# The 16 by 16 corners of the attention probabilities: turned on VectorE in 32 by 32 blocks instead of on TensorE, with GpSimd's low parts of weights in 128-column pieces

## The chip, the cores and the metric

One core of a Trainium2 chip runs the whole program. The metric is the device time of one execution in microseconds. Before the change it is 1282.98 us, the median of three runs (1282.68 to 1283.24).

## What is computed

Two layers of a decoder over 528 positions: 16 learned meta tokens and then 512 real ones, of width 1024. Each layer projects the normed input once and gives its columns to eight heads of forgetting attention (64 wide) and four heads of retention (128 wide); their outputs are joined, projected and added to h; a gated feed-forward of width 2816 follows. The part that matters here is the attention:

```python
def attend(q_blk, c_q, q_pos, k_, v_, c_k, k_pos):
    s = jnp.einsum('bhqd,bhkd->bhqk', q_blk, k_).astype(jnp.float32) * scale
    s = s + c_q[..., :, None] - c_k[..., None, :]
    s = jnp.where(k_pos[None, :] <= q_pos[:, None], s, -jnp.inf)
    p = jax.nn.softmax(s, axis=-1)
    return jnp.einsum('bhqk,bhkd->bhqd', p.astype(v_.dtype), v_)

meta_out = attend(...)      # the 16 meta queries, a block of their own
# the 512 real queries, in 4 blocks of 128
h = h + jnp.einsum('blc,cd->bld', mix, w_out)
```

A query sees the keys up to its own position. A block of 128 real queries begins at position 16 + 128 b, and key tiles of 128 begin at 0, 128, 256, 384 and 512. So query block b needs the key tiles 0 to b, and of key tile b + 1 only its first 16 keys, and those only for the last 16 queries of the block: a 16 by 16 corner, whose upper triangle is masked.

## The kernel before, in words

Activations lie with features on the 128 partitions and the 528 positions along the free axis. Every product is computed in three parts from operands that are split into a high part (rounded to a matmul format) and a low part (the rest): high x high, high x low, low x high. So weights and activations are split all the time, the high part by a copy on ScalarE and the low part by a subtraction on VectorE (`split`, L126 to L128).

**Weights.** `dense_steps` gives a projection of 128 output columns as eight steps, one for each slice of 128 inputs; a step is six matmuls of 264 columns (or three of 512). Weights come by DMA into `raw`, and `convert` (L150) splits them in halves of four slices, 128x512 elements each: ScalarE writes `whi` (L176), and GpSimd (in the jobs marked `pool`) or VectorE writes `wlo` (L177). It is called one job ahead, at steps 1 and 4 of the job before.

**Attention.** Heads go in four pairs g (s = 0, 1). `scores(s, b)` computes the scores of one query block into PSUM, adds the mask to the diagonal piece on VectorE (L496), subtracts the cumulated gates and takes the row minimum (L497, into the tile `pd` of this block; L502 joins two minima for block 3), and ScalarE takes the exponential in place (L510). The meta block, b = -1, exists in layer 0 alone and has its own tiles `pm`; `normalise` (L520) divides it by its sums.

`turn(s, b)` (L526) brings the probabilities into the form that the second product needs, keys on the partitions: TensorE transposes the 128-column tiles of the block against the identity into PSUM, up to four to a bank (L401 in `transpose_into`), and `split` writes `pth` on ScalarE (L127) and `ptl` on VectorE (L128), which are [key in tile, key tile, query]. Block b is turned in b + 2 tiles, the last of which holds only the corner; the columns behind it are zeros, written once per layer. So block 3 takes five transposes and two splits. The meta block takes one transpose of a whole 128x128 tile.

`product(s)` (L536) multiplies with the values (L544 for the meta queries, L552 for the real ones); key tile j is used for the queries from 128 j on.

**Order.** TensorE's order is written by hand: `merge` places the steps of attention and retention among the projections' steps, and `turn` stands three blocks behind `scores`. The other engines' instructions are put in order by a scheduler, except those that are pinned; each engine then runs its own list in order. Work on SBUF by GpSimd and VectorE goes on while TensorE multiplies.

Of the kernel before, what the change touches and what calls it, by code (L numbers as in the profile page):

```python
# [10 lines left out]
F32 = mybir.dt.float32  # L11
# [7 lines left out]
META = 16  # L19
T = SEQ + META  # L20
# [12 lines left out]
GAMMA = tuple(1.0 - 2.0 ** (-5 - h) for h in range(RH))  # L33
NEG = -1.0e30
HALF = T // 2


@with_exitstack
def hybrid_kernel(ctx, tc, x_t, w_in, w_fl, w_out, w_gate, w_up, w_down, vecs, b_fg, rope, decay, mask, ident, out_t):
    nc = tc.nc  # L40
# [22 lines left out]
    onec = const.tile([128, 1], F32, name="onec")  # L63
    nc.vector.memset(onec, 1.0)

    p_tiles, pm_tiles, v_tiles, end_tiles, low_keys = [], [], [], [], []
    rot = {"pm": 0}


# [10 lines left out]
    def enter_att(l):  # L80
        enter("att")
        low_keys[:] = [phase["att"].tile([128, T], F32R, name=f"kl{s}") for s in range(2)]
        for s, t in enumerate(low_keys):
            (nc.gpsimd if l else nc.vector).memset(t[64 * (1 - s):64 * (2 - s)].bitcast(F32), 0.0)

        for lst, n, cols, z0 in ((p_tiles, NBLK, None, None), (v_tiles, 2, TP, T)):
            lst[:] = [phase["att"].tile([128, cols or 128 * (i + 2)], F32, name=f"pd{z0}_{i}") for i in range(n)]
            for i, t in enumerate(lst):
                z = META + 128 * (i + 1) if z0 is None else z0
                zero(l, t[:, z:z + 128 - META])  # L90
        pm_tiles[:] = [phase["att"].tile([128, 128], F32, name=f"pm{i}") for i in range(2)] if l == 0 else []
        for t in pm_tiles:
            zero(l, t)
        end_tiles[:] = [[phase["att"].tile([128, META], F32R, name=f"rs{i}{k}") for k in range(2)] for i in range(2)]
        for t in end_tiles[0] + end_tiles[1]:
            zero(l, t.bitcast(F32))

    def zero(l, t):
        (nc.gpsimd if l else nc.vector).memset(t, 0.0)
# [50 lines left out]
    def convert(j, upto=NK, pinned=False):  # L150
# [18 lines left out]
        while job["split"] < min(n, upto):  # L169
            c0 = job["split"]  # L170
            c1 = min(n, c0 + (2 if j < 2 and c0 < 4 else 4))
            size, hi, lo = job["w"][c0 // job["w"][0][0]]
            o = c0 % size
            hi, lo = hi[:, o:o + c1 - c0], lo[:, o:o + c1 - c0]
            with tc.high_priority() if j == 5 else ExitStack():
                pin(nc.scalar.copy(hi, job["raw"][:, c0:c1]), pinned)  # L176
            pin(sub(lo, job["raw"][:, c0:c1], hi.bitcast(F32)), pinned)  # L177
# [112 lines left out]
    def pin(f, pinned=True):  # L290
        if pinned:
            tc.keep_in_program_order(f)
# [160 lines left out]
    def fox_steps(g, st, ly, real):  # L453
# [21 lines left out]
        def scores(s, b):  # L475
# [33 lines left out]
            pr = pt[0:nq, 0:nk]  # L509
            nc.scalar.activation(pr, pr, AF.Exp, bias=nmax[0:nq], scale=-1.0, accum_out=rsum)  # L510
# [69 lines left out]
        steps.append(lambda: product(1))  # L580
        cut = len(steps) - lag - 1
        return steps[:cut], steps[cut:]

    KOFF = (0, 128, 256, 384, SEQ)
    KLEN = (128, 128, 128, 128, META)
# [798 lines left out]
```

## Time and profile before

| | before |
|---|---|
| median of the runs | 1282.98 us |
| the profiled execution, first to last instruction (span) | 1282.4 us |
| TensorE busy | 1265.5 us, 9335 matmuls |
| VectorE busy | 1013.6 us, 1828 instructions |
| ScalarE busy | 691.4 us, 1246 instructions |
| GpSimd busy | 177.3 us, 145 instructions |

The profile is of one execution; no time of its own is given for it beside its span, which is 0.6 us below the median of the runs. PE is TensorE's matmul (a transpose is one too), PEld its weight load, DVE VectorE, ACT ScalarE, POOL GpSimd. Matmuls overlap, so the distance between the starts of two tells more than how long one lasts. A bracket behind a row of the timeline names how long the engine was idle before it, and what ended that.

### The profile page before, as it was taken

Reading aid. Unit: us, or ns where it says so; the run is one execution under the profiler, and the core shown is the slowest. Engines: PE = TensorE matmul, PEld = TensorE weight load, DVE = VectorE, ACT = ScalarE, POOL = GpSimd, SP = SyncE. Lnnn points to the kernel's source line nnn. Section 1 sums busy time; section 2 is a strip of 40 time slices with the busy share of each in tenths; the row PEclk is TensorE's granted clock in tenths of the full one; section 3 lists DMA queues with packets and bytes.
Section 4 is the critical chain, followed back from the end, with each engine's and each line's share of the span. In section 5 each row is a group of like instructions: output and inputs, shape, how many; then the busy total and the mean of one; then the engine's idle time right before and its main releaser. Section 6 shows DMA issues by size and latency. Waiting matters only on the chain.

```text
span 1282.4 us, 23297 instructions
## 1 busy us (share of the span) xinstructions
PE 1265.5 (99%) x9335; PEld 1205.4 (94%) x9335; DVE 1013.6 (79%) x1828; ACT 691.4 (54%) x1246; POOL 177.3 (14%) x145
## 2 busy tenths in 40 slices
PE   9999999999999999999999999999999999999997
PEld 8899999999999999999999989999789999999996
DVE  7877856879988887887686878568899878888866
ACT  6666655676444444444455665457765444444444
POOL 1233333210000000000014334333000000000000
PEclk9999999999999999999999999999999999999998
DMA  6222222123333333332323122222223322332321
GB/s 231 76 67 84 75 84 84 60 68 121 109 98 99 99 99 99 100 99 83 99 76 117 59 99 84 75 92 67 99 78 129 106 99 99 99 100 99 105 77 66
DMA packets 45676, 120.54 MB, mean 94 GB/s; under 512 B 5360, under 2 KB 12272, under 8 KB 45568
## 3 DMA queue, kind: packets, MB, share of 16 engines
q1 hardware_dynamic: 45136, 118.77, 28.2%
q8 instruction: 73, 1.20, 0.4%
q14 instruction: 35, 0.29, 0.1%
q10 hardware_dynamic: 432, 0.29, 0.1%
HBM read 116.91 MB, written 2.13 MB: 93 GB/s over the span
## 4 chain that ended last, share of the span: by engine, by line
PE 88%; DVE 7%; ACT 3%; DMA 1%; issue 1%; DVEq 0%; ACTq 0%
PE psd L200 27%; PE psa L860 18%; PE psd L995 14%; PE psd L860 13%; PE psa L995 4%; PE psa L200 4%; PE psa L401 2%; PE psa L490 2%; PE psa L552 1%; PE psa L709 1%; PE psa L679 1%; DMA bc<-cdr 1%; ACT whi L176 0%; DVE qs L421 0%; DVE kl L435 0%
## 5 line engine op out<-in xcount | busy, mean ns | idle before, releaser
L177 POOL TENSOR_TENSOR wlo<-raw,whi 128x512 fp32r<-128x512 f32 x126 | 171.8, 1377 | 386.0 <-ACT whi L176 384.8
L200 PE MATMUL psd<-xh,whi 128*128 128x264 f32 (+1 forms) x792 | 196.6, 316 | 0.8 <-ACT whi L176 0.8
L200 PE MATMUL psd<-xh,wlo 128*128 128x264 f32 (+1 forms) x792 | 187.2, 304 | 0.0
L200 PE MATMUL psd<-xl,whi 128*128 128x264 f32 (+1 forms) x792 | 186.5, 303 | 0.4 <-DVE xl L303 0.4
L200 PEld LDWEIGHTS psd<-xh,whi 128*128 128x128 f32 x792 | 128.9, 190 | 5.6 <-ACT whi L176 1.5
L200 PEld LDWEIGHTS psd<-xh,wlo 128*128 128x128 f32 x792 | 127.5, 189 | 6.4 <-DVE wlo L177 0.4
L200 PEld LDWEIGHTS psd<-xl,whi 128*128 128x128 f32 x792 | 128.2, 190 | 4.7 <-DVE xl L303 0.8
L176 ACT CAST whi<-raw 128x512 fp32r<-128x512 f32 (+1 forms) x168 | 98.2, 614 | 38.2 <-PE psd L200 18.0
L848 ACT CAST whi<-raw 128x1024 fp32r<-128x1024 f32 (+2 forms) x62 | 54.9, 885 | 51.3 <-PE psd L860 40.0
L848 ACT CAST fwhi<-raw 128x1024 fp32r<-128x1024 f32 (+2 forms) x62 | 55.6, 897 | 47.5 <-PE psd L860 40.0
L849 DVE TENSOR_TENSOR wlo<-raw,whi 128x1024 fp32r<-128x1024 f32 (+2 forms) x62 | 62.9, 1014 | 11.3 <-ACT whi L848 10.9
L849 DVE TENSOR_TENSOR fwlo<-raw,fwhi 128x1024 fp32r<-128x1024 f32 (+2 forms) x62 | 64.0, 1032 | 9.0 <-ACT fwhi L848 8.7
L860 PE MATMUL psa<-th,whi 128*128 128x264 f32 (+1 forms) x232 | 65.5, 282 | 0.0
L860 PE MATMUL psa<-th,wlo 128*128 128x264 f32 (+1 forms) x232 | 65.4, 282 | 0.0
L860 PE MATMUL psa<-tl,whi 128*128 128x264 f32 (+1 forms) x232 | 65.3, 282 | 0.0
L510 ACT ACTIVATE pdNone<-pdNone,nmax 128x144 f32<-128x144 f32 (+1 forms) x64 | 36.9, 576 | 50.4 <-DVE nmax L497 33.6
L860 PE MATMUL psa<-th,fwhi 128*128 128x264 f32 (+1 forms) x224 | 63.4, 283 | 0.0
L860 PE MATMUL psa<-tl,fwhi 128*128 128x264 f32 (+1 forms) x224 | 63.3, 283 | 0.0
L860 PE MATMUL psa<-th,fwlo 128*128 128x264 f32 (+1 forms) x224 | 63.3, 282 | 0.0
L128 DVE TENSOR_TENSOR ptl<-psa,pth 128x512 fp32r<-128x512 f32 (+4 forms) x88 | 41.9, 490 | 26.9 <-ACT pth L127 26.9
L926 ACT COPY e<-psa 128x264 f32<-128x264 f32 (+1 forms) x114 | 42.8, 375 | 28.4 <-PE psa L860 24.1
L848 ACT CAST fwhi<-S 128x1024 fp32r<-128x1024 f32 x20 | 21.0, 1049 | 68.6 <-PE psa L860 66.5
(339 smaller groups left out, 4031.7 us busy)
## 6 DMA issues: line engine op xcount, KB each, us to landing
raw<-w_in SPq DMA_DIRECT2D x54, 512.0 KB, 3.5
raw<-w_gate SPq DMA_DIRECT2D x44, 512.0 KB, 3.9
fraw<-w_up SPq DMA_DIRECT2D x38, 512.0 KB, 3.5
raw<-w_down SPq DMA_DIRECT2D x64, 256.0 KB, 2.7
raw<-w_out SPq DMA_DIRECT2D x16, 512.0 KB, 3.5
raw<-w_down SPq DMA_DIRECT2D x32, 192.0 KB, 2.4
bc<-cdr SPq DMA_DIRECT2D x16, 264.0 KB, 3.2
raw<-w_up SPq DMA_DIRECT2D x6, 512.0 KB, 3.4
```

What stands on the lines that cost most here:

```text
L128: pin(nc.vector.tensor_sub(lo, src, hi.bitcast(F32)), pinned)
L176: pin(nc.scalar.copy(hi, job["raw"][:, c0:c1]), pinned)
L177: pin(sub(lo, job["raw"][:, c0:c1], hi.bitcast(F32)), pinned)
L200: nc.tensor.matmul(ps[1][b][:, 0:c1 - c0], w[:, wk, :], x[:, c0:c1], start=(k == 0 and i == 0), stop=(k == n - 1 and i == 2))
L401: nc.tensor.transpose(ps[:, 128 * j:128 * j + 128], src[:, o:o + 128], idt)
L490: nc.tensor.matmul(sc[0:nq, 0:c1 - c0], st["q"][s][:, q0:q0 + nq], kk[:, c0:c1], start=(i == 0), stop=(i == 1))
L510: nc.scalar.activation(pr, pr, AF.Exp, bias=nmax[0:nq], scale=-1.0, accum_out=rsum)
L848: nc.scalar.copy(hi, src)
L849: nc.vector.tensor_sub(lo, src, hi.bitcast(F32))
L860: nc.tensor.matmul(bank()[:, 0:b.shape[-1]], a[:, o + k, :], b, start=(fresh and k == 0 and i == 0), stop=(k == n - 1 and i == 2), skip_gr ...
L926: nc.scalar.copy(self.t["e"][:, i], self.t["x"][:, 0:w])
L995: nc.tensor.matmul(v[:, 0:c1 - c0], a[:, s * n + k, :], b[:, c0:c1], start=(k == 0 and i == 0), stop=(k == n - 1 and i == 2))
```

## The change

It has two parts.

*Corners.* `turn` transposes b + 1 tiles of a real block on TensorE instead of b + 2, and none of the meta block. The four corners of a head lie in rows 112 to 127 of the four `pd` tiles; these become slices of one tile, at a distance (`PSTEP`) at which one access pattern reaches the four 32x32 blocks in rows 96 to 127. One VectorE instruction (`nc.vector.transpose`, STREAM_TRANSPOSE in the order) turns all four into the tile `corner`, and one `split` of 32x4x16 writes them to `pth` and `ptl` in `turn(s, 3)`. The instruction for head s stands ahead of the next head's first scores (`cut_corners`), since those overwrite block 0's tile. The meta block is turned in a 32x32 block of its own, and its tiles shrink to 32x32. `pth` and `ptl` are now taken once a layer and not once a pair of heads; GpSimd zeroes the 16-column stripes of the corners in them, once a layer.

*Pieces.* The low part of a half of the weights is written by GpSimd in four instructions of 128 columns and not one of 512. VectorE's stay as they were.

```diff
@@ convert
+            wide = 1 if job["pool"] else c1 - c0
+            for i in range(0, c1 - c0, wide):
+                pin(sub(lo[:, i:i + wide], job["raw"][:, c0 + i:c0 + i + wide], hi[:, i:i + wide].bitcast(F32)), pinned)
-            pin(sub(lo, job["raw"][:, c0:c1], hi.bitcast(F32)), pinned)
@@ scores
             normalise()
+            cut_corners()
...
+            if b == NBLK - 1:
+                info["cut"] = s
@@
+        def cut_corners():
+            if "cut" in info:
+                t = info["corner", info.pop("cut")] = corner_tile(NBLK)
+                nc.vector.transpose(t, corner_blocks(p_tiles[NBLK]))
+
+        def corner_tile(n):
+            return at("corner", F32, (32, NBLK, 32), 3)[:, 0:n]
@@ turn
+            if not turned:
+                turned[:] = [at(n, shape=(128, 5 * T)) for n in ("pth", "ptl")]
+                for t in turned:
+                    zero(1, corners(t, 0, 5).bitcast(F32))
             if b == blocks[0]:
-                st["pt"] = (at("pth", shape=(128, 5, T)), at("ptl", shape=(128, 5, T)))
+                st["pt"] = [t.rearrange("p (j q) -> p j q", j=5) for t in turned]
...
-            for j0, n, p3 in transpose_into(info[s, b], [128 * j for j in range(b + 2)]):
+            for j0, n, p3 in transpose_into(info[s, b], [128 * j for j in range(b + 1)]) if b >= 0 else []:
                 split(pth[:, j0:j0 + n, q0:q0 + nq], ptl[:, j0:j0 + n, q0:q0 + nq], p3[:, :, 0:nq])
+            if b in (-1, NBLK - 1):
+                j0, n, c0 = (0, 1, 0) if b < 0 else (1, NBLK, 32 - META)
+                if b < 0:
+                    t = corner_tile(1)
+                    nc.vector.transpose(t, info[s, b].unsqueeze(1))
+                else:
+                    cut_corners()
+                    t = info["corner", s]
+                split(corners(turned[0], j0, n)[0:32], corners(turned[1], j0, n)[0:32], t[:, :, c0:c0 + META])
```

What moves on the engines. TensorE in layer 0, first pair of heads, around `turn(1, 3)`, the block of five tiles (L679 and L719 are retention's scores); before:

```order
L200 MATMUL psd<-xh_196,whi 128x264 x2
L200 MATMUL psd<-xl_197,whi 128x264 x2
L200 MATMUL psd<-xh_196,wlo 128x264 x2
L401 MATMUL psa<-idt,pdNone_108 128x128 x5
L679 MATMUL psa<-rqh,rkh 128x272
```

and after, at the same place:

```order
L206 MATMUL psd<-xh_193,whi 128x264 x2
L206 MATMUL psd<-xl_194,whi 128x264 x2
L206 MATMUL psd<-xh_193,wlo 128x264 x2
L407 MATMUL psa<-idt,pd 128x128 x4
L719 MATMUL psa<-rqh,rkh 128x272
```

One transpose has gone and nothing else has moved. VectorE in layer 0, first pair, from the second head's first minimum on (tq and rql are of retention, L128 and L132 are the low parts of splits); before:

```order
L128 TENSOR_TENSOR ptl<-psa,pth 128x3x128
L128 TENSOR_TENSOR rql<-tq,rqh 128x528
L496 TENSOR_TENSOR psa<-psa,msk 128x128
L523 RECIPROCAL rsum<-rsum 16x1
L497 ISA pdNone_105,nmax<-psa,bc 128x144
L497 ISA nmax 128x1
L524 TENSOR_SCALAR pm_118<-pm_118,rsum 16x16
L128 TENSOR_TENSOR ptl<-psa,pth 128x4x128
```

and after:

```order
L538 STREAM_TRANSPOSE corner<-pd 32x128
L132 TENSOR_TENSOR ptl<-psa,pth 128x2x128
L503 TENSOR_TENSOR psa<-psa,msk 128x128
L132 TENSOR_TENSOR rql<-tq,rqh 128x528
L504 ISA pd,nmax<-psa,bc 128x144
L504 ISA nmax 128x1
L532 RECIPROCAL rsum<-rsum 16x1
L132 TENSOR_TENSOR ptl<-corner,pth 32x4x16
L533 TENSOR_SCALAR pm_115<-pm_115,rsum 16x16
L132 TENSOR_TENSOR ptl<-psa,pth 128x3x128
```

The turn of the first head's corners stands ahead of the minimum that overwrites block 0's tile, and the splits carry one tile less each. GpSimd from its first weights to the start of layer 1; before:

```order
L347 MEMSET pth 128x1024
L177 ISA
L177 TENSOR_TENSOR wlo<-raw,whi 128x512 x62
L84 MEMSET kl_8267 64x528
```

and after:

```order
L353 MEMSET pth 128x1024
L183 ISA
L183 TENSOR_TENSOR wlo<-raw,whi 128x128 x4
L103 MEMSET pth 128x5x16
L183 TENSOR_TENSOR wlo<-raw,whi 128x128 x12
L103 MEMSET ptl 128x5x16
L183 TENSOR_TENSOR wlo<-raw,whi 128x128 x232
L85 MEMSET kl_8414 64x528
```

The 62 halves have become 248 pieces, and the two zeroings of the corner stripes stand among the first of them.

More of the change, by code (lines that the diff above doesn't have):

```diff
@@ L35 @@
 HALF = T // 2
+PSTEP = 416
 @with_exitstack
@@ L64, in hybrid_kernel @@
     nc.vector.memset(onec, 1.0)
-    p_tiles, pm_tiles, v_tiles, end_tiles, low_keys = [], [], [], [], []
+    p_tiles, pm_tiles, v_tiles, end_tiles, low_keys, turned = [], [], [], [], [], []
     rot = {"pm": 0}
@@ L84, in enter_att @@
             (nc.gpsimd if l else nc.vector).memset(t[64 * (1 - s):64 * (2 - s)].bitcast(F32), 0.0)
[L86 to L91, printed above, removed]
+        pd = phase["att"].tile([128, PSTEP * (NBLK - 1) + 128 * NBLK + 32], F32, name="pd")
+        p_tiles[:] = [pd[:, PSTEP * i:PSTEP * i + 128 * (i + 1) + 32] for i in range(NBLK)] + [pd]
+        for i, t in enumerate(p_tiles[:NBLK]):
+            zero(l, t[:, 128 * (i + 1) + META:128 * (i + 1) + 32])
+        v_tiles[:] = [phase["att"].tile([128, TP], F32, name=f"vd{i}") for i in range(2)]
+        for t in v_tiles:
+            zero(l, t[:, T:TP])
+        turned[:] = []
+        pm_tiles[:] = [phase["att"].tile([32, 32], F32, name=f"pm{i}") for i in range(2)] if l == 0 else []
         for t in pm_tiles:
@@ L582, in fox_steps, with blocks_of, corners, corner_blocks @@
         return steps[:cut], steps[cut:]
+    def blocks_of(t, first, n, step, width):
+        v = t[:, first:first + 1]
+        return bass.AP(v.tensor, v.offset, [list(v.ap[0]), [step, n], [1, width]])
+    def corners(t, j0, n):
+        return blocks_of(t, j0 * (T + 128), n, T + 128, META)
+    def corner_blocks(t):
+        return blocks_of(t, 128, NBLK, PSTEP + 128, 32)[96:128]
     KOFF = (0, 128, 256, 384, SEQ)
```

## The prediction

> **What bounds the kernel now.** I read the page's busy shares first, then what TensorE waited for, in the list of waits for that engine. The busy shares:
>
> ```profile
> PE 1265.5 (99%) x9335; PEld 1205.4 (94%) x9335; DVE 1013.6 (79%) x1828; ACT 691.4 (54%) x1246; POOL 177.3 (14%) x145
> ...
> POOL 1233333210000000000014334333000000000000
> ```
>
> The second row is GpSimd's busy share in 40 slices of 32 us: its 17 slices above zero, some 545 us, are the attention stages of the two layers, where the whole change lies. TensorE is at work in 1265.5 of 1282.4 us, so an instruction taken from it is worth its issue time, unless a wait grows in its place. The waits in the attention stages, each with total us, times, longest:
>
> ```profile
> PE psa L552 <- DVE ptl L128: 1.2, 1, 1.2
> PE psa L401 <- DVE pd L441: 0.9, 1, 0.9
> ...
> PE psa L490 <- DVE kl L435: 0.6, 1, 0.6
> PE psa L401 <- DVE vv L467: 0.5, 1, 0.5
> PE psa L490 <- DVE nmax L497: 0.4, 1, 0.4
> ...
> PE psa L490 <- DVE mixt L556: 0.3, 1, 0.3
> PE psd L200 <- DVE h L763: 0.3, 1, 0.3
> ```
>
> Seven waits, 4.2 us together, every one for VectorE. This is all that a quicker VectorE can give. The times of the runs have a median of 1282.98, 0.6 us above this execution's span; I add my differences to the median, since nothing in the change lies outside the span.
>
> **Part one: the transposes that go.** How many there are, and what they take in the stream (start, us, engine and line):
>
> ```profile
> L401 PE MATMUL psa<-idt,pdNone x224: 270/272/328, 47.4 to 889.4; 128*128 128x128 f32 x112
> L401 PE MATMUL psa<-idt,pm x8: 270/272/328, 44.3 to 245.0; 128*128 128x128 f32 x8
> ```
> ```profile
> 54.88 0.71 PE L401 MATMUL psa<-idt,pdNone 128*128 128x128 f32 x5
> ...
> 55.35 0.48 PE L200 MATMUL psd<-xh,whi 128*128 128x264 f32 x2
> ...
> 55.67 0.41 PE L200 MATMUL psd<-xl,whi 128*128 128x264 f32 x2
> ...
> 55.92 0.40 PE L200 MATMUL psd<-xh,wlo 128*128 128x264 f32 x2
> ```
> ```profile
> 101.76 0.27 PE L401 MATMUL psa<-idt,pm 128*128 128x128 f32 x1
> 101.79 0.49 PE L200 MATMUL psd<-xh,whi 128*128 128x264 f32 x2
> 102.12 0.41 PE L200 MATMUL psd<-xl,whi 128*128 128x264 f32 x2
> ```
>
> One transpose lasts 272 ns, but TensorE overlaps them, so the price is the distance between starts. A pair of 264-column matmuls takes 55.92 - 55.67 = 0.25 us. Five transposes and one pair take 55.67 - 54.88 = 0.79 us, so five take 0.54 and one takes 0.11. A lone one: 102.12 - 101.76 - 0.25 = 0.11. The price is the same in a group and alone.
>
> Each head loses the last transpose of its blocks 0 to 3, and in layer 0 also the one of the meta block: 8 heads x 5 + 8 heads x 4 = 72. 72 x 0.11 = 7.9 us off TensorE's stream. Nothing is added there: the corners are turned on VectorE, and the finer waits for GpSimd's pieces ride on matmuls.
>
> TensorE: Matmul & The Clock Gate, a page of the Trainium skill (Part 4, PE-mode transpose), gives about 275 ns for a transpose within a kernel; by that figure the sum would be 72 x 0.275 = 19.8 us, an estimate. The rows here have that duration and yet a spacing of 0.11, so I go by the spacing; the larger price is a rival below.
>
> **Part two: what VectorE and ScalarE do instead.** Rows of VectorE and ScalarE around one block 3 in layer 0:
>
> ```profile
> 161.80 0.16 DVE L128 TENSOR_TENSOR ptl<-psa,pth 128x16 fp32r<-128x16 f32 x1
> ...
> 162.63 0.29 DVE L496 TENSOR_TENSOR psa<-psa,msk 128x128 f32<-128x128 f32 x1
> ...
> 164.75 0.42 DVE L128 TENSOR_TENSOR ptl<-psa,pth 128x256 fp32r<-128x256 f32 x1 [1.15 <-ACT pth L127]
> ...
> 167.90 0.54 DVE L128 TENSOR_TENSOR ptl<-psa,pth 128x384 fp32r<-128x384 f32 x1
> ```
> ```profile
> 163.63 0.74 ACT L510 ACTIVATE pdNone<-pdNone,nmax 128x528 f32<-128x528 f32 x1 [2.17 <-DVE nmax L502]
> ```
>
> The splits of blocks 0, 1 and 2 shrink by 128 columns, 0.54 - 0.42 = 0.12 us each on VectorE: 48 x 0.12 = 5.8 us less. Block 3's second split (128x128) becomes the corner split (32x64), the meta block's (128x16) becomes 32x16: about even. Added are 24 block turns (16 of 32x128, 8 of 32x32), an operation that no row shows. Its bounds are the smallest VectorE row, 0.16, and the 384-column row, 0.54: 3.8 to 13 us. I take 0.29, the row with 128 elements a partition: 7.0 us. VectorE's work thus stays the same within some 7 us of 545, in which it has idle time (the rows of the windows below: 60% busy); I cost it at nothing on the path. If that cover were gone, it would be 7 us.
>
> The change adds a wait: the turn of a head's four corners stands on VectorE behind the exponential of block 3, ahead of the next head's first mask and minimum, and in the output projection's stretch an addition to h is queued behind it, for which TensorE could wait. But the row at 164.75 shows VectorE idle at this very place today, 1.15 us, until ScalarE had done the exponential of 163.63 and a copy after it. The new wait ends no later than that idle time did: nothing, and at most 0.74 us, the exponential's length, where other work fills that place.
>
> **Part three: GpSimd in pieces.** VectorE and GpSimd hold each other up, shown by all engines' rows around the wait for L441 and the one for L552:
>
> ```profile
> 85.49 0.70 DVE L734 SCALAR_TENSOR_TENSOR ge<-ge,gr 128x528 f32<-128x528 f32 x1
> 85.62 3.43 POOL L177 TENSOR_TENSOR wlo<-raw,whi 128x512 fp32r<-128x512 f32 x2 [6.68 <-ACT whi L176]
> ...
> 86.23 1.68 DVE L735 SCALAR_TENSOR_TENSOR gr<-ge,gr 128x528 f32<-128x528 f32 x1
> ...
> 92.46 1.83 POOL L177 TENSOR_TENSOR wlo<-raw,whi 128x512 fp32r<-128x512 f32 x1 [3.41 <-ACT whi L176]
> ...
> 93.17 1.69 DVE L283 SCALAR_TENSOR_TENSOR r<-nwt,r 128x528 f32<-128x528 f32 x1
> ...
> 96.06 0.89 PE L401 MATMUL psa<-idt,pd 128*128 128x128 f32 x5 [0.87 <-DVE pd L441]
> ```
> ```profile
> 58.19 1.28 POOL L177 TENSOR_TENSOR wlo<-raw,whi 128x512 fp32r<-128x512 f32 x1 [2.05 <-ACT whi L176]
> ...
> 58.77 1.26 DVE L598 TENSOR_TENSOR tq<-tq,xsw 128x528 f32<-128x528 f32 x1
> ...
> 60.69 0.50 PE L552 MATMUL psa<-ptl,vv 128*128 128x512 f32 x1 [1.21 <-DVE ptl L128]
> ```
>
> L735 and L283 are of L734's form and take 1.68 and 1.69 in place of 0.70 while a GpSimd instruction runs; L598, of the same size, takes 1.26, 0.56 more. Such an operation sits out the rest of a 1.3 us instruction. After the change it sits out the rest of a piece. A piece's price:
>
> ```profile
> L177 POOL TENSOR_TENSOR wlo<-raw,whi 128x512 fp32r<-128x512 f32 x126 | 171.8, 1377 | 386.0 <-ACT whi L176 384.8
> ```
> ```profile
> L347 POOL MEMSET pth<- 128x1024 f32 x2 | 1.9, 954 | 0.3 <-POOLq L1372 0.3
> ...
> L99 POOL MEMSET pdNone<- 128x112 f32 x4 | 0.6, 185 | 0.0
> ```
> ```profile
> L177 POOL TENSOR_TENSOR wlo<-raw,whi x126: 1267/1294/2897, 21.6 to 906.8; 128x512 fp32r<-128x512 f32 x126
> ...
>   PEld psa L200: 0.4, 1
> ```
> ```profile
> 165.00:200.00 35.00, 35.00 (x288) 34.82 (x288) 21.16 (x49) 18.38 (x42) 13.15 (x10) 1.00 0.23 75
> 800.00:860.00 60.00, 59.99 (x394) 54.46 (x393) 34.90 (x79) 30.86 (x68) 23.44 (x18) 1.00 0.24 82
> ```
>
> At least a quarter of 1294, 0.32 us. The two memsets give 0.84 ns a column and 91 ns fixed; with 0.09 fixed a piece takes 0.09 + 1.20/4 = 0.39, four take 1.56 instead of 1.29. The windows' columns are the stretch, its length, and the busy time of TensorE, its weight loads, VectorE, ScalarE and GpSimd, with counts. In the densest stretch, 800 to 860, 18 x 1.56 = 28 of 60 us: GpSimd keeps up. TensorE has waited for it once, 0.4 us, on the weight loads' row, and its first 128 columns now come after 0.39 instead of 1.29. The pieces cost nothing there and shorten VectorE's stalls from up to 1.3 to up to 0.4, some 0.2 on average.
>
> **The sum on the path.** The transposes: -7.9. The wait for ptl at 60.69 swallows the first head's five, since the chain before it runs through VectorE and not TensorE: +0.55. In that chain L598's stall falls from 0.56 to 0.2: -0.36. In the chain to 96.06 two stalls of 0.98 fall to 0.2 each, more than the wait of 0.87: it goes, -0.87. TensorE, up to 0.55 us earlier at each head's end, will meet new short waits; I take two of the size of the rows above, 0.3 to 0.4: +0.7. Together -7.9: 1282.98 - 7.9 = **1275.1**.
>
> **Rivals.**
> *GpSimd becomes the bound (slower).* A VectorE operation can also hold up a GpSimd one: at 92.46 it took 1.83. If VectorE gets between all pieces with 0.70 each, a piece costs 0.39 + 0.70 = 1.09 and four 4.36 us. Then 800 to 860 needs 18 x 4.36 = 78 us (+18) and 165 to 200 needs 44 (+9): 1275.1 + 27 = 1302. It decides from 60 / (18 x 4) = 0.83 us a piece. Against it: 1377 mean over 1267 lowest is only 0.11 us of such blocking an instruction, and VectorE is busy only some 60% of those two stretches. Chance 0.05. The page SBUF — State Buffer of the Trainium skill (Who interferes with whom) states as a rule that of VectorE and GpSimd whichever starts first holds the port pair that they share for its whole instruction, and that the other blocks fully. By that rule, with which the stalls above agree, each piece can be blocked afresh, where one instruction of 512 columns is blocked once.
> *The saved time is swallowed.* Each head's chain through ScalarE and VectorE sets the pace, and its wait grows by what TensorE saves, as at 60.69: about 1282. Against it: only seven waits stand in 545 us of attention. Chance 0.07.
> *The pieces don't free VectorE*, since GpSimd runs all four before VectorE gets in: no relief (+1.2), and stalls of up to 1.56 instead of 1.29, some 1 to 2 us more: 1278. Against it: the two instructions from 85.62 take 3.43 instead of 2.6, and L735 ended at 87.91, about 1.1 us before the second did, so the two alternate. Chance 0.08.
> *A transpose is worth its 272 ns:* 72 x 0.272 = 19.6, 1263.4. Against it: the spacing in the two groups above. Chance 0.02.
>
> **How the numbers follow.** My forecast has 0.76; 0.02 is left for what I didn't think of, on the fast side. The low end is the transposes and all 4.2 us of waits: 1282.98 - 7.9 - 4.2 = 1270.9. The high end is half of the saving swallowed (4.0) and the longer wait at 60.69: 1282.98 - 7.9 + 4.5 = 1279.6, which holds the third rival. Outside lie the first, second and fourth rivals, and the rest of 0.02: 0.16. What this measurement can tell from no change is about 0.2%, 2.6 us. Faster by more: 0.76 + 0.08 + 0.02 + 0.02 = 0.88. Within it: 0.06, the most of the second rival. Slower: 0.05 + 0.01 = 0.06.
>
> **What would show it.** Right: 232 transposes of the p tiles and pm become 160, TensorE's busy time falls by about 8 us, the transposes still stand 0.11 apart; L735 and L283's likes at no more than 1.1 us; the wait for pd gone, the one for ptl still there; GpSimd's pieces at 0.32 to 0.5 us. Wrong: rows of TensorE waiting for GpSimd's wlo (first rival); the sum of TensorE's waits up by 4 us or more (second); VectorE operations still at 1.7 us (third); STREAM_TRANSPOSE over 0.54 us, or VectorE's waits for the exponential with additions to h late behind them, would break part two.

## The result, and the profile after

The changed kernel takes 1272.44 us (median of 4 runs, 1272.19 to 1272.66), beside 1283.11 of the kernel before on the same chip: a ratio of 0.9913 (95% interval 0.9899 to 0.9927), some 11 us faster. The forecast was 1275.1 in a range of 1270.9 to 1279.6: the sign and the range hold, the gain is 3 us larger than its sum.

The page of the kernel after: busy shares, GpSimd's 40 slices, and GpSimd's group (busy us, mean ns, idle before).

```profile
PE 1253.3 (99%) x9263; PEld 1195.1 (94%) x9263; DVE 998.6 (79%) x1852; ACT 687.3 (54%) x1246; POOL 266.9 (21%) x527
...
POOL 3455545410000000000025546454100000000000
...
L183 POOL TENSOR_TENSOR wlo<-raw,whi 128x128 fp32r<-128x128 f32 x504 | 261.4, 554 | 270.0 <-ACT whi L180 250.0
```

TensorE has 72 instructions less and is 12.2 us less busy; VectorE has 24 more and is 15 us less busy. So VectorE was freed, though it got work: it no longer sits beside long GpSimd instructions. GpSimd itself is at work half as long again as before (177.3 us). What TensorE waits for now:

```profile
PE psa L407 <- DVE vv L473: 1.8, 1, 1.8
...
PE psa L497 <- DVE kl L441: 0.9, 1, 0.9
PE psa L582 <- DVE ptl L132: 0.8, 1, 0.8
PE psa L497 <- DVE nmax L504: 0.7, 1, 0.7
...
PE psa L497 <- DVE mixt L586: 0.5, 1, 0.5
PE psa L407 <- DVE nmax L504: 0.5, 1, 0.5
```

The waits for pd and h are gone, the one for ptl is smaller, none is for GpSimd; but the one for vv grew from 0.5 to 1.8, and together these six come to 5.2 us, where the seven of before came to 4.2. So this list alone does not show the gain. Where the time went is seen best in two views that I use for every kernel below. The first is the row of one tile, TensorE's matmuls `psa<-th,wlo`. Its first start is in layer 0's feed-forward, just behind the attention, and its last one at the end of layer 1's; so the first number holds layer 0's attention and the distance between the two holds layer 1's. Before, then after:

```profile
L860 PE MATMUL psa<-th,wlo x232: 279/281/289, 336.7 to 1243.1; 128*128 128x264 f32 x58, 128*128 128x256 f32 x58
```
```profile
L900 PE MATMUL psa<-th,wlo x232: 279/281/288, 328.1 to 1232.1; 128*128 128x264 f32 x58, 128*128 128x256 f32 x58
```

By this row layer 0 gave 8.6 us. One of them lies ahead of its attention: the first scores of 272 columns start at 40.83 before and at 39.86 after, so from there on layer 0 gave 7.6. From the feed-forward on it took 1243.1 - 336.7 = 906.4 before and takes 904.0 now: layer 1 gave only 2.4, less than its 32 transposes at 0.11 (3.5). The second view is the busy time in two stretches, layer 0's attention from its first scores on and the later part of layer 1's (columns as in the prediction). Before, then after:

```profile
42.00:340.00 298.00, 294.89 (x2399) 291.48 (x2398) 234.78 (x518) 182.19 (x386) 75.26 (x56) 1.00 0.25 82
700.00:940.00 240.00, 239.49 (x1480) 212.71 (x1479) 180.80 (x372) 147.32 (x298) 71.21 (x53) 1.00 0.25 84
```
```profile
42.00:340.00 298.00, 296.69 (x2423) 294.41 (x2421) 234.37 (x540) 183.21 (x389) 117.48 (x224) 1.00 0.26 83
700.00:940.00 240.00, 239.56 (x1463) 212.74 (x1462) 179.88 (x382) 148.29 (x297) 104.84 (x207) 1.00 0.27 85
```

TensorE's idle time in the first stretch falls from 298 - 294.89 = 3.1 to 1.3 us. In the second there was hardly any to win, 0.5 before and 0.4 now.

### The profile page after: what moved, and what is told of

Read it like the earlier page. It is cut to its first block, busy times and chain, and to the rows that moved or that the text cites. A ratio compares the mean times of both kernels' runs of the same rounds, so it can differ in the third digit from the quotient of the medians.

```text
span 1270.6 us, 23600 instructions
## 1 busy us (share of the span) xinstructions
PE 1253.3 (99%) x9263; PEld 1195.1 (94%) x9263; DVE 998.6 (79%) x1852; ACT 687.3 (54%) x1246; POOL 266.9 (21%) x527
## 4 chain that ended last, share of the span: by engine, by line
PE 93%; DVE 2%; ACT 2%; DMA 2%; issue 0%; SPq 0%; DVEq 0%; ACTq 0%
PE psd L206 29%; PE psa L900 19%; PE psd L1035 14%; PE psd L900 13%; PE psa L206 5%; PE psa L1035 4%; PE psa L407 2%; PE psa L582 2%; PE psa L497 2%; PE psa L749 1%; PE psa L719 1%; DMA bc<-cdr 1%; DMA h<-x_t 0%; DMA cdr<-z 0%; PE psa L279 0%
## 5 line engine op out<-in xcount | busy, mean ns | idle before, releaser
L183 POOL TENSOR_TENSOR wlo<-raw,whi 128x128 fp32r<-128x128 f32 x504 | 261.4, 554 | 270.0 <-ACT whi L180 250.0
L889 DVE TENSOR_TENSOR wlo<-raw,whi 128x1024 fp32r<-128x1024 f32 (+2 forms) x62 | 62.9, 1015 | 12.8 <-ACT whi L888 12.7
L889 DVE TENSOR_TENSOR fwlo<-raw,fwhi 128x1024 fp32r<-128x1024 f32 (+2 forms) x62 | 64.0, 1032 | 10.5 <-ACT fwhi L888 10.1
L517 ACT ACTIVATE pd<-pd,nmax 128x144 f32<-128x144 f32 (+1 forms) x64 | 36.9, 576 | 43.8 <-DVE nmax L504 31.8
```

The costliest lines, as they stand in the source:

```text
L183: pin(sub(lo[:, i:i + wide], job["raw"][:, c0 + i:c0 + i + wide], hi[:, i:i + wide].bitcast(F32)), pinned)
L889: nc.vector.tensor_sub(lo, src, hi.bitcast(F32))
```

## The experiments

The theories on record, made once the result and its profile were known: A, the forecast's terms; B, a transpose is worth more than its spacing and the pieces are worth nothing; C, the pieces give much and cost about 2 us where layer 1 begins. C came from SyncE's queue there. SyncE's DMA issues, VectorE's scan that makes the gates' sums, and VectorE's first use of their broadcast (start, us; in the bracket the idle time before). Before, then after:

```profile
663.09 12.72 SPq L143 DMA_DIRECT2D raw<-w_in  x2
...
671.47 2.23 DVE L382 TENSOR_TENSOR_SCAN z<-z 8x528 f32<-8x528 f32 x1
...
675.86 0.32 SPq L384 DMA_DIRECT2D cdr<-z  x1
...
678.86 1.41 SPq L480 DMA_DIRECT2D bc<-cdr  x2
...
682.29 0.31 DVE L497 CUSTOM_DVE_ANT_0 pdNone<-psa,bc 128x144 f32<-128x144 f32 x1 [1.83 <-DMA bc<-cdr]
```
```profile
655.78 12.64 SPq L147 DMA_DIRECT2D raw<-w_in  x2
...
662.76 1.40 DVE L388 TENSOR_TENSOR_SCAN z<-z 8x528 f32<-8x528 f32 x1
...
668.47 0.32 SPq L390 DMA_DIRECT2D cdr<-z  x1
...
671.68 0.81 SPq L486 DMA_DIRECT2D bc<-cdr  x2
...
675.70 0.31 DVE L504 CUSTOM_DVE_ANT_0 pd<-psa,bc 128x144 f32<-128x144 f32 x1 [3.88 <-DMA bc<-cdr]
```

The sums are copied to memory (`cdr`) and read back as a broadcast (`bc`). In both kernels the copy's issue follows at once on a row of raw-weight loads that lasts 12.7 us because its second load waits for a buffer. The scan is done 2.2 us before the copy starts in the kernel before (673.70 to 675.86), and 4.3 us in the kernel after (664.16 to 668.47); VectorE then idles 1.83 and 3.88 us. What the buffer waits for, SyncE's waits for GpSimd (total, times, longest), before and after:

```profile
SPq L143 <- POOL wlo L177: 400.4, 62, 15.3
```
```profile
SPq L147 <- POOL wlo L183: 185.6, 60, 5.9
```

These totals fall, so the place, not the sum, tells the story. The load just ahead of the copy waits for GpSimd last in both kernels: 12.0 us before, 5.0 us after. At the layer's start GpSimd works through 16 pieces without a gap, and they last longer than four whole runs. Before, then after:

```profile
671.29 7.13 POOL L177 TENSOR_TENSOR wlo<-raw,whi 128x512 fp32r<-128x512 f32 x4 [8.23 <-ACT whi L176]
```
```profile
662.58 8.84 POOL L183 TENSOR_TENSOR wlo<-raw,whi 128x128 fp32r<-128x128 f32 x16 [6.72 <-ACT whi L180]
```

Counted from GpSimd's start there, the copy starts 4.6 us later before (675.86 - 671.29) and 5.9 us later after (668.47 - 662.58). So the pieces hold the copy back by 1.3 us; the other 0.8 by which the copy now lags the scan is that the scan is done sooner (2.4 us from GpSimd's start before, 1.6 after).

All runs stand in this table (medians in us; start is the first `psa<-th,wlo`, rest the distance to its last; idle is TensorE's in 42 to 340). A ratio is to runs of before on the same chip, whose medians lie between 1282.92 and 1283.90, and differences to before go by those:

| kernel | median (runs) | ratio to before, 95% | start | rest | idle |
|---|---|---|---|---|---|
| before | 1283.11 (4) | | 336.7 | 906.4 | 3.1 |
| after | 1272.44 (4) | 0.9913, 0.9899 to 0.9927 | 328.1 | 904.0 | 1.3 |
| after, again | 1272.41 (4) | 0.9912, 0.9899 to 0.9926 | 329.3 | 902.9 | 1.3 |
| corners alone | 1276.70 (5) | 0.9947, 0.9934 to 0.9961 | 332.4 | 902.6 | 4.9 |
| pieces alone | 1281.23 (11) | 0.9981, 0.9972 to 0.9990 | 333.6 | 909.1 | 1.6 |
| corners, pieces of 256 | 1275.30 (5) | 0.9937, 0.9924 to 0.9949 | 333.3 | 902.9 | 3.4 |
| corners, pieces of 64 | 1281.39 (12) | 0.9982, 0.9973 to 0.9990 | 332.1 | 905.8 | 3.1 |
| after, 64 transposes twice | 1280.32 (11) | 0.9974, 0.9966 to 0.9983 | 332.7 | 907.1 | 1.2 |
| after, corners not turned | 1273.35 (5) | 0.9921, 0.9908 to 0.9935 | 328.3 | 903.3 | 1.2 |
| before, copy on ScalarE's queue | 1282.82 (11) | 0.9994, 0.9985 to 1.0003 | 337.1 | 905.8 | 3.1 |
| after, copy on ScalarE's queue | 1270.60 (4) | 0.9899, 0.9886 to 0.9913 | 328.9 | 901.4 | 1.3 |
| after, copy and broadcasts there | 1270.30 (4) | 0.9898, 0.9883 to 0.9912 | 328.2 | 901.3 | 1.3 |
| corners, pieces of 64, both there | 1272.03 (5) | 0.9913, 0.9899 to 0.9927 | 330.0 | 901.8 | 1.8 |
| corners alone, both there | 1276.11 (5) | 0.9943, 0.9929 to 0.9956 | 332.1 | 902.3 | 3.9 |

The start column differs by 1.2 us between two profiles of one kernel, the rest column by 1.1; smaller differences in them say nothing. TensorE's clock is in these columns as well, in two ways. At the program's start it is lower: pairs of 264-column matmuls stand 0.44 us apart for some microseconds and 0.24 from then on: up to about 10.3 us in the profile of before, 10.5 in the repeat of the kernel after, 5.5 in its first profile. The 1.2 us stand ahead of the attention: the scores that start at 39.86 in the first profile start at 41.00 in the repeat, and from there to the feed-forward they take 288.2 and 288.3. And in four of the profiles the granted clock falls once more for a moment, which takes 1.7 us: with pieces alone and with pieces of 64 at about 685 (in the rest column), with pieces of 256 and with pieces of 64 and both DMAs moved at about 60 (in the start column). The row of pieces alone, with the granted clock third from the end, gives 5 x (1 - 0.66) = 1.7:

```profile
685.00:690.00 5.00, 4.24 (x17) 3.62 (x17) 4.14 (x15) 1.10 (x5) 0.00 (x0) 0.66 0.27 105
```

What brings these stretches no run here isolates.

### Each part by itself, and the kernel after once more

Corners alone leaves the low parts whole; pieces alone is the kernel before with the new loop in `convert`; the third halves the number of pieces.

```diff
# corners alone, against after
-            wide = 1 if job["pool"] else c1 - c0
+            wide = c1 - c0
# pieces alone, against before
-            pin(sub(lo, job["raw"][:, c0:c1], hi.bitcast(F32)), pinned)
+            wide = 1 if job["pool"] else c1 - c0
+            for i in range(0, c1 - c0, wide):
+                pin(sub(lo[:, i:i + wide], job["raw"][:, c0 + i:c0 + i + wide], hi[:, i:i + wide].bitcast(F32)), pinned)
# pieces of 256, against after
-            wide = 1 if job["pool"] else c1 - c0
+            wide = 2 if job["pool"] else c1 - c0
```

> The corners alone, GpSimd's halves left at 512 columns. Theory A (the forecast's terms): the transposes give 7.9 us, the wait for ptl in the first pair of heads takes 0.55 back, and the waits that the pieces would relieve stay: about 7 us faster than before, ratio 0.9945 (0.993 to 0.996), with VectorE operations of 1.6 to 1.7 us still in the trace. Theory B (a transpose is worth more than its spacing, and the pieces are worth nothing): the whole 10.6 us, ratio 0.9915 to 0.992. Theory C (the pieces give much and also cost 2 us where layer 1 begins): as A, and the wait of TensorE for the values' split there is back to about 0.5 us.

> The pieces alone, all transposes left on TensorE. Theory A: 1.2 us faster than before, ratio 0.999 (0.998 to 1.000). Theory B: no change, 1.000. Theory C: 3 to 4 us gained over the attention stages by shorter stalls of VectorE, and about 2 us lost where layer 1 begins, since SyncE's queue holds the copy of the gates' sums back behind a load of raw weights that waits for GpSimd's pieces: ratio 0.997 to 0.999, and the trace shows the copy of cdr in layer 1 issued 4 us or so after the scan's end.

> The changed kernel with GpSimd's pieces of 256 columns. A piece of 128 takes 0.46 us and one of 512 took 1.29, which puts 256 at 0.74, two at 1.48 beside four at 1.85. Theory A: a stall of VectorE is up to 0.74 and not 0.46, so 0.3 to 0.5 us slower than the changed kernel: ratio to before 0.992. Theory B: same as the changed kernel. Theory C: GpSimd's first eight pieces of layer 1 end about 1.5 us earlier, TensorE's wait there shrinks by about 1 us, and the stalls take about 0.5 back: 0.5 us faster than the changed kernel, ratio to before 0.991.

> The changed kernel itself, beside the others on the same chip: 0.9913 to 0.992 of before by its first timing. Its profile shows a second time whether the full TensorE clock comes at 5.2 us from the start, as in the changed kernel's profile, or at 10.3 us, as in that of before. If it belongs to the change, it is 5.2 again here and 10.3 where the start of the program is that of before; if it varies from run to run, it does neither.

The repeat of the kernel after comes out at 1272.41, and its full clock comes about as late as in before, so that is no part of the change: it varies from run to run.

Corners alone is 6.9 us faster, as A has it. But 72 transposes at 0.11 are 7.9, and TensorE idles longer than before. The stretch 42 to 340 of corners alone, and its waits:

```profile
42.00:340.00 298.00, 293.14 (x2384) 289.79 (x2383) 239.96 (x533) 181.01 (x384) 75.61 (x56) 1.00 0.25 81
```
```profile
PE psa L582 <- DVE ptl L132: 1.5, 1, 1.5
...
PE psa L407 <- DVE psa L503: 1.2, 1, 1.2
PE psd L206 <- DVE h L803: 1.0, 1, 1.0
```

4.9 us of idle time against 3.1, at waits that the profile before had smaller (ptl 1.2, h 0.3) or not at all (the masked scores of L503). A faster TensorE runs into VectorE. Pieces alone show the other half:

```profile
42.00:340.00 298.00, 296.38 (x2421) 293.92 (x2420) 228.31 (x520) 183.32 (x387) 118.11 (x224) 1.00 0.26 82
```
```profile
L862 PE MATMUL psa<-th,wlo x232: 279/281/288, 333.6 to 1242.7; 128*128 128x264 f32 x58, 128*128 128x256 f32 x58
```

Layer 0's idle time is halved, but the rest takes 909.1 us, 2.7 more than before. Of these 1.7 are the stretch of lower clock, in a profile of the slowest of the eleven runs (1282.98, the median 1281.23). So layer 1 as a whole loses 1.0 us, no more than two profiles differ by. But where it begins TensorE waits 0.7 us for nmax and 1.8 for vv, 2.0 more than the 0.5 of before, and the copy's place is that of the kernel after (the scan ends at 669.71, the copy starts at 674.03). So both parts of C hold, and B falls; the ratio alone, 0.9981, lies in A's range as well as in C's.

The pieces do this without a new order: TensorE, ScalarE and VectorE run the same instructions in the same order in corners alone and in the kernel after, and in before and pieces alone. The corners do change it: with them some 200 of VectorE's 1852 instructions stand elsewhere in its list.

The two parts gain more together than apart, 11.2 against 6.9 + 2.4, since corners alone lose 1.8 us to waits that the pieces take away.

Pieces of 256 were to be 0.3 to 0.5 us slower than pieces of 128 by A and 0.5 faster by C's detail. They are 2.9 us slower, so both are wrong there, and their idle time lies in between.

### Pricing a transpose, and VectorE's new work

```diff
# 64 transposes twice, against after: the last tile of each real block
-                nc.tensor.transpose(ps[:, 128 * j:128 * j + 128], src[:, o:o + 128], idt)
+                for _ in range(2 if again and o == offs[-1] else 1):
+                    nc.tensor.transpose(ps[:, 128 * j:128 * j + 128], src[:, o:o + 128], idt)
# corners not turned, against after
-                t = info["corner", info.pop("cut")] = corner_tile(NBLK)
-                nc.vector.transpose(t, corner_blocks(p_tiles[NBLK]))
+                info.pop("cut")
...
-            if b in (-1, NBLK - 1):
+            if b in ():
```

> The kernel after, with the last transpose of each of the real blocks issued a second time (64 transposes more, same data to the same place). Prices the transpose on the path. By the spacing in a row (0.11 us each, theory A): +7.0 us, 1279.5. By its full duration of 0.27 us each (theory B): +17.4 us, 1289.8. Where TensorE waits behind it anyhow, less: a sum of +4 to +5 would say that a third of what the change removed from TensorE was swallowed by waits and that the rest came from VectorE's shorter stalls.

> The kernel after without VectorE's turns of the corners (24 block turns) and without the two halves of each corner copied from them: the corners of the turned probabilities stay zero, so that part of the attention is left out. Prices VectorE's added work. By the forecast's steps it costs nothing on the path: within 0.5 us of the kernel after. If VectorE is what TensorE waits for around the first blocks (waits for ptl 0.8, nmax 0.7 and 0.5, mixt 0.5), 1 to 2 us faster.

64 more transposes cost 1280.32 - 1272.44 = 7.9 us, 0.12 each; from the ends of the two ratios' intervals, 5 to 11 us, 0.08 to 0.17. The spacing of 0.11 is right and the duration of 0.27 is not. Beside the repeat of the kernel after, whose full clock came about as late at the start, it is 3.4 us for the 32 of layer 0 (start column) and 4.2 for the 32 of layer 1 (rest column). Not turning the corners, in a kernel that leaves out that part of the attention, gains nothing (1273.35, 0.9 slower, with intervals that overlap): VectorE's added work is hidden, as forecast.

### The queue at the start of a layer

The copy of the sums is issued from ScalarE's queue, in the kernel after and, as a control, in the kernel before; then the broadcasts too.

```diff
-        nc.sync.dma_start(st["cdr"], z2)
+        nc.scalar.dma_start(st["cdr"], z2)
# copy and broadcasts: this as well
-                nc.sync.dma_start(bc, ly["cdr"][hd:hd + 1, :].partition_broadcast(128))
+                nc.scalar.dma_start(bc, ly["cdr"][hd:hd + 1, :].partition_broadcast(128))
```

> The kernel after, with the copy of the gates' sums to memory (cdr) issued from ScalarE's queue and not from SyncE's. Theory C (the pieces cost about 2 us where layer 1 begins, since this copy stands on SyncE's queue behind a load of raw weights that waits for a buffer which GpSimd's pieces free): the copy starts within 0.7 us of the end of VectorE's scan, the wait for vv (1.8 us) shrinks below 0.9 and the kernel comes to 1270.4 to 1271.6 us, 0.9 to 2 us under the kernel after. Rival D (the queue's place is chance: something else, the broadcast's own transfer or ScalarE's work ahead of the copy, sets that wait): within 0.4 us of the kernel after, with the same wait for vv or another in its place.

> The control: the kernel before with the same edit. Between the scan's end (673.70) and the copy's issue (675.86) lie 2.2 us there. If the place on SyncE's queue costs time in the kernel before too, it gains up to 1.5 us, and the loss is not the pieces' own but older than they are; by theory C in its narrow form (the pieces brought it) the kernel before stays within 0.4 us.

> The kernel after with the copy of the gates' sums and the broadcasts read back from it (bc) both issued from ScalarE's queue. With the copy alone moved, the first broadcast still stood on SyncE's queue until 669.32, when the raw-weight load ahead of it was issued, though the copy was on its way from 665.02, and VectorE waited 0.89 us for it. If what was left of the loss is that queue: the broadcast starts at about 667.8 and up to 0.9 us more are gained, 1269.7 to 1270.5 us. Rival (ScalarE's own queue is held up by the broadcast's wait for the copy, 2.5 us or so, and its casts and exponentials come late): 1 to 3 us slower than with the copy alone, with TensorE's waits on ScalarE (whi L180, sqh) longer.

Same rows as above, of the kernel after with the copy on ScalarE's queue:

```profile
656.62 12.65 SPq L147 DMA_DIRECT2D raw<-w_in  x2
...
663.60 1.40 DVE L388 TENSOR_TENSOR_SCAN z<-z 8x528 f32<-8x528 f32 x1
...
665.02 0.28 ACTq L390 DMA_DIRECT2D cdr<-z  x1
...
669.32 0.90 SPq L486 DMA_DIRECT2D bc<-cdr  x2
...
673.56 0.31 DVE L504 CUSTOM_DVE_ANT_0 pd<-psa,bc 128x144 f32<-128x144 f32 x1 [0.89 <-DMA bc<-cdr]
```

The copy now starts 0.02 us after the scan, VectorE idles 0.89 in place of 3.88, TensorE's wait for vv has left the list, and the kernel takes 1270.60 us (1270.44 to 1271.08), 1.8 less than after, whose eight runs all lie above 1272.1. C holds in the gain, though not all of the 1.8 is the pieces'. In the kernel before, the same edit gives a ratio of 0.9994 (0.8 us) whose interval touches no change, and the rest column falls by 0.6. So the place on the queue cost little, if anything, before the pieces came, and some 1.0 to 1.2 us of the 1.8 are the pieces' own, as the 1.3 us above have it.

With the broadcasts moved as well, the first starts at 665.76 and that wait of VectorE is gone, but 1270.30 can't be told from 1270.60: the 0.9 us that were still seen there were not on TensorE's path. ScalarE was not held up either.

### Smaller pieces

```diff
# pieces of 64, against after
-            wide = 1 if job["pool"] else c1 - c0
-            for i in range(0, c1 - c0, wide):
-                pin(sub(lo[:, i:i + wide], job["raw"][:, c0 + i:c0 + i + wide], hi[:, i:i + wide].bitcast(F32)), pinned)
+            parts = [(i, h) for i in range(c1 - c0) for h in (0, 64)] if job["pool"] else []
+            if not parts:
+                pin(sub(lo, job["raw"][:, c0:c1], hi.bitcast(F32)), pinned)
+            for i, h in parts:
+                pin(sub(lo[:, i, h:h + 64], job["raw"][:, c0 + i, h:h + 64], hi[:, i, h:h + 64].bitcast(F32)), pinned)
```

> The kernel after, with GpSimd's low parts in pieces of 64 columns (eight for a run of 512). So far, with the corners turned by VectorE: 512 columns 1276.7, 256 columns 1275.3, 128 columns 1272.4 us; GpSimd busy 36 of 60 us at 0.55 us a piece of 128. Theory A with the forecast's first rival (finer is better for VectorE until GpSimd becomes the bound, 0.83 us for 128 columns): a piece of 64 at 0.35 to 0.40 us makes 0.7 to 0.8 us for 128 columns, near the point where it decides: within 1 us of the kernel after if it stays below, 5 to 25 us slower and TensorE waiting for wlo in stages of matmuls if it goes above. Theory E (the gain is only VectorE's shorter stall, and goes on with the size): 1 to 2 us faster.

Nine us slower than pieces of 128. E falls, and at first sight the forecast's first rival is there. But GpSimd is busy 41.59 of the 60 us from 800 to 860, and TensorE never waits for wlo. The loss that its profile shows stands first at the start of layer 0, where GpSimd works without a gap:

```profile
24.07 12.29 POOL L185 TENSOR_TENSOR wlo<-raw,whi 128x64 fp32r<-128x64 f32 x24
...
26.36 10.34 SPq L147 DMA_DIRECT2D raw<-w_in  x2
...
34.34 1.24 DVE L390 TENSOR_TENSOR_SCAN z<-z 8x528 f32<-8x528 f32 x1
...
36.80 0.30 SPq L392 DMA_DIRECT2D cdr<-z  x1
...
43.47 0.16 DVE L506 CUSTOM_DVE_ANT_0 pm<-psa,bc 16x16 f32<-16x16 f32 x1 [4.58 <-DMA bc<-cdr]
```
```profile
PE psa L499 <- DVE nmax L506: 3.5, 1, 3.5
```

The same chain again: pieces, a buffer, SyncE's queue, the copy, the broadcast, and TensorE's wait for the minimum, 3.5 us where the kernel after has 0.7. At layer 1's start the wait for vv is 1.8 as in the kernel after, and what is added there is lower clock: 0.83 granted from 680 to 690, 1.7 us.

The profile is of the fastest of the twelve runs, 1278.17, and the median is 3.2 us above it. The runs' mean granted clocks are 0.992 to 0.996, on average 0.0033 below those of the kernel after's eight (0.995 to 0.999). Over 1281 us that is about 4 us, an estimate: so nearly half of the nine us is a lower clock and not waiting. Whether the waits bring it, no run isolates.

The test is to change the queue of the copy and of the broadcasts:

```diff
-        nc.sync.dma_start(st["cdr"], z2)
+        nc.scalar.dma_start(st["cdr"], z2)
...
-                nc.sync.dma_start(bc, ly["cdr"][hd:hd + 1, :].partition_broadcast(128))
+                nc.scalar.dma_start(bc, ly["cdr"][hd:hd + 1, :].partition_broadcast(128))
```

> The kernel with the corners turned and pieces of 64 columns (1281.4 us, 9 slower than the kernel after), with the copy of the gates' sums and the broadcasts issued from ScalarE's queue. In its trace the loss stands at two places only: 2.5 us at 41 (VectorE waited 4.58 us for the broadcast there) and 2.6 at 660 to 690, besides a clock halved for 3.4 us. Theory C (the queue behind the weights is the whole cost of small pieces; GpSimd's own rate is not a bound even at 0.39 us a piece): 1270 to 1273 us, within 2 us of the same kernel with pieces of 128. Rival (GpSimd's rate holds the weights back where a layer begins): 1275 us or more, with TensorE waiting for wlo or whi there.

> Corners turned by VectorE, low parts still in whole runs of 512 columns (1276.7 us), with the copy and the broadcasts issued from ScalarE's queue. If the pieces' part in the gain (4.3 us from 1276.7 to 1272.4) is VectorE's shorter stalls all along the stage, it stays: 1274.5 to 1276.5 us, 4 to 6 us above the kernel with pieces of 128 and the same queue (1270.3). Rival (the pieces only shift when the queue is free): within 2 us of 1270.3.

Pieces of 64 come to 1272.03 us: about 9 us back, with GpSimd's instructions as long as they were (0.39 us mean) and the clock of four of the five runs at 0.997 or 0.998, of the fifth at 0.999. So GpSimd's rate was not the bound; the queue was, and the clock's part went with it. The edit is not the queue alone: the scheduler also puts some 60 of VectorE's 1852 instructions and some 50 of ScalarE's 1246 at another place. But it does so in corners alone too, where the same edit gives 0.6 us. Corners alone on that queue stay at 1276.11, so the pieces of 128 are worth 1276.11 - 1270.30 = 5.8 us there, between two kernels whose TensorE and ScalarE run the same list and whose VectorE's list differs at two places alone. They do not merely shift when the queue is free. The remaining 1.7 us between pieces of 64 and of 128 stand at one place of the profiles: the wait for ptl at about 58 is 0.8 us longer (1.6 for 64 columns, 0.8 for 128), and behind it the granted clock is 0.83 from 55 to 65, another 1.7 us in that run; why, no run here isolates.

## Why the prediction was right, and where it was off

**The transposes: -7.9.** Right. 160 are left, and five still start 0.11 apart (0.71 = 0.27 + 4 x 0.11):

```profile
L407 PE MATMUL psa<-idt,pd x160: 270/272/328, 46.0 to 878.7; 128*128 128x128 f32 x160
```
```profile
91.52 0.71 PE L407 MATMUL psa<-idt,vd 128*128 128x128 f32 x5
```

Issued twice, they cost 0.12 each on the whole time. The Trainium skill gives about 275 ns for a transpose within a kernel (TensorE: Matmul & The Clock Gate, Part 4, PE-mode transpose): the row's duration agrees at 272, and yet it is no price on a pipelined stream.

**Swallowed by the first head's wait: +0.55, and two new short waits: +0.7.** Near for corners alone, in the sum, and by luck: 7.9 less 6.9 is 1.0, against 1.25. The waits were others than foreseen: ptl grew by 0.3 and not 0.55, and those for L503's masked scores and for h grew by 1.9 together.

**VectorE's corner turns: nothing.** Right: leaving them out gains nothing. The block turn of 32x128 took what was assumed, 0.30 against 0.29, and the smaller one less:

```profile
L538 DVE STREAM_TRANSPOSE corner<-pd x16: 302/302/304, 49.6 to 867.3; 32x128 f32<-32x128 f32 x16
L560 DVE STREAM_TRANSPOSE corner<-pm x8: 189/199/200, 41.6 to 216.5; 32x32 f32<-32x32 f32 x8
```

The bound for the new wait behind the exponential was too small: VectorE idled up to 1.5 us there, not 0.74, without cost. That holds with the pieces; corners alone had the wait for h, 1.0 us, that the forecast named as the danger.

**A piece: 0.39 us.** Too low: 0.46 median, 0.55 mean. The forecast took the fixed part, 0.09, from memsets. The four sizes have medians of 322, 463, 742 and 1294 ns for 64 to 512 columns: (1294 - 463) / 384 = 2.16 ns a column and 463 - 128 x 2.16 = 186 ns fixed. The Trainium skill (GPSIMD Engine Reference, Elementwise — side-by-side cycle accounting) gives GpSimd about 2.6 cycles an element in a two-input operation; at the 1.2 GHz of the page's own sum that is 2.17 ns, an estimate, and the slope measured here agrees.

**VectorE's stalls fall to 0.4.** Right, and better than said. The operations of the prediction and their likes, shortest, median, longest; before, then after:

```profile
L735 DVE SCALAR_TENSOR_TENSOR gr<-ge,gr x4: 692/1186/1679, 86.2 to 779.7; 128x528 f32<-128x528 f32 x2, 128x512 f32<-128x512 f32 x2
...
L598 DVE TENSOR_TENSOR tq<-tq,xsw x16: 680/1032/1692, 50.1 to 876.4; 128x528 f32<-128x528 f32 x12, 128x512 f32<-128x512 f32 x4
...
L283 DVE SCALAR_TENSOR_TENSOR r<-nwt,r x8: 671/692/1771, 93.2 to 905.0; 128x528 f32<-128x528 f32 x4, 128x512 f32<-128x512 f32 x4
```
```profile
L775 DVE SCALAR_TENSOR_TENSOR gr<-ge,gr x4: 692/700/708, 81.8 to 770.6; 128x528 f32<-128x528 f32 x2, 128x512 f32<-128x512 f32 x2
...
L638 DVE TENSOR_TENSOR tq<-tq,xsw x16: 683/709/1018, 48.9 to 866.1; 128x528 f32<-128x528 f32 x12, 128x512 f32<-128x512 f32 x4
...
L289 DVE SCALAR_TENSOR_TENSOR r<-nwt,r x8: 675/700/858, 88.5 to 893.8; 128x528 f32<-128x528 f32 x4, 128x512 f32<-128x512 f32 x4
```

Of these none is above 1.02 us, against 1.69 and 1.77, and of all of VectorE's operations of 128x528 none is above 1.03. The Trainium skill's rule that the blocked engine waits for the other's whole instruction (SBUF — State Buffer, Who interferes with whom) fits that; the rival that was drawn from it, GpSimd blocked afresh at each piece, would need over 0.83 us a piece, and the mean is 0.55.

**What the pieces give: about half a microsecond** (-0.36 and -0.87, against +0.7). Wrong. This is the term that was mis-sized: beside the corners they gave 1276.70 - 1272.44 = 4.3 us, and 5.8 with the queue moved. The step that failed is the sentence that the seven waits, 4.2 us, are all that a quicker VectorE can give, of which only two were then counted. A list of waits is no fixed store: corners alone raised TensorE's idle time in layer 0 from 3.1 to 4.9 us, and the pieces took it to 1.3, which is 3.6 us. The forecast saw that a faster TensorE would meet new waits, and did not credit the pieces with removing them. That the sum came within 3 us all the same owes something to luck, two misses of opposite sign: the pieces gave more than was said, and the queue took back something that was put at nothing.

**The pieces cost nothing on GpSimd.** Right where it looked, in the dense stretches; wrong at the layer's start. GpSimd's last read frees the raw buffer, the load that waits for it stands on SyncE's queue, and the copy of the sums stands behind it. The forecast followed GpSimd to TensorE and not to the queue that it releases. With the copy on another queue the kernel after gains 1.8 us; 0.6 to 0.8 of that place's cost are there without pieces too, and 1.0 to 1.2 are what the pieces took from the gain.

The terms in order, from the traces: layer 0, 40 transposes at 0.11 to 0.12 (4.4 to 4.8) and 1.8 of idle time make 6.2 to 6.6, where 7.6 went from the first scores on. Part of the missing microsecond is in how a wait is counted: idle time begins at the end of the last matmul, and matmuls overlap. The wait for h, before:

```profile
156.66 0.40 PE L200 MATMUL psd<-mxh,wlo 128*128 128x264 f32 x2
157.35 0.51 PE L200 MATMUL psd<-mxh,whi 128*128 128x264 f32 x2 [0.28 <-DVE h L763]
```

The starts are 0.69 us apart in place of 0.24, so the wait costs 0.45 where 0.28 are listed. In the same way the wait for pd costs 1.02 (0.87 listed) and one for sql at 85.63 costs 0.45 (0.23). These three are gone after, and make 0.5 us more than their idle time; the rest of the microsecond stays without a cause that was shown. So the 4.2 us of the forecast were short from the start. Layer 1, 32 transposes, 3.5 to 3.8, less up to about a microsecond at its start: the rest column shows 2.4 and 3.5, and 5.0 with the copy moved.

## What to carry to other kernels

Two edits that touch the same wait are priced together: shortening one engine's stream exposes the waits that the other edit removes. Where an edit changes when an engine is done with its input, follow the buffer that it frees to the DMA that waits for it, and then read what else stands behind that DMA on its queue; here one small copy cost 1.8 us in one kernel, and with its broadcasts 9 us in another, some 4 of them by a lower clock; issuing them from another queue gave both back. A wait costs the distance between starts that it adds, which is more than the idle time listed for it. Where two profiles of one kernel are compared, the clock in each is read first. Piece size has a floor, which the fixed cost of an instruction argues for: 128 columns were better here than 256 and, at the start of a layer, than 64. The kernel after with the copy issued from ScalarE's queue is the fastest but for noise, at 1270.3 to 1270.6 us.

## What was not expected of the hardware

A GpSimd subtraction costs 186 ns and 2.16 ns for each fp32 column, twice the fixed part of its memset (91 ns). VectorE's scan, 8x528, took 2.23 us beside whole runs of GpSimd and 1.40 beside pieces. A transpose that has a duration of 272 ns is worth 0.12 us of the kernel's time.
